# Sums formed in the up stage, a seventh raw tile, and the in projection's small matmuls set apart in stages

## The chip, the cores and the metric

The kernel runs on one core of a Trainium2 chip. The metric is the device time of one execution in microseconds; times are compared as medians of several runs. The engines are TensorE (PE, with its weight loads PEld), VectorE (DVE), ScalarE (ACT), GpSimd (POOL), and SyncE (SP), whose queue issues most of the DMAs.

## What is computed

One inference step of a decoder layer in float32, for 512 prompt tokens and 64 sample tokens (8 sequences of 8), model width 2048:

```python
h = rms_norm(x, norm1)
proj = h @ w_in                       # 2048 x 7168
ya = gate_b * causal_dwconv(gate_c * xa)                 # short convolution, 512 columns
yb = dilated_attention(...)           # 3 groups x 4 heads x 128, windows 128/512/2048, dilations 1/4/16
yc = multiscale_pool(...)             # 4 groups x 256, trailing means over 2/4/8/16, a map per group
x = x + concat(ya, yb, yc) @ w_out
h2 = rms_norm(x, norm2)
x = x + (silu(causal_dwconv(h2 @ w_gate)) * (h2 @ w_up)) @ w_down     # D_FF = 5504
y = rms_norm(x, final_norm)
```

The sample tokens also read caches of keys and values (to 2048 rows per sequence), pool and convolution states, and the updated caches and states are outputs too.

## The kernel before

**Layout.** Activations stand transposed: 128 channels on the partitions, 576 tokens (512 + 64) along the free dimension, in two halves of 288. Each float32 operand is split into a high part (rounded to the matmul's format, by ScalarE) and a low part (the rest, by VectorE); a product is the sum of three matmuls, high by high, high by low and low by high, each 128 x 128 by 128 x 288. `wload` (L146) and `split_w` (L930) split weights so.

**In projection** (up to about 880 us). `project` (L180) makes one block of 128 columns in two units of eight k-tiles, 48 matmuls each, and calls `tick` (L656) after each unit. `tick` runs the functions that `post(delay, fn)` (L644) has put on that tick, then lets two queues of generators go on, the sample tokens' scores (L473) and values (L530). Four heads of nine blocks each run (`head_tiles`, L673), with four pooling blocks behind the second and third head (`pool_tiles`, L727) and twelve blocks of the short convolution at the end. One tick after a head's last block `att_prompt` (L381) is written out whole: for each of four query tiles scores, mask, softmax, transposes, values, transpose. A pooling block is followed one tick later by its state rows (`state_rows`, L718) and, every second block, by `pool_map` (L771), whose operands are `dtl` tiles split into slots "ek", which the sample keys use too. The pool state is loaded right before its transpose (L737). The sample values are summed by `collect` (L566): a group of small matmuls into a PSUM bank, and VectorE adds the bank to `ob` (L572, L574). PSUM has two "ps" banks, one "s" and one "pt" for all these small things, and two accumulators `acc`.

**Out projection** (to about 1120 us), then **gate and up** with `strassen_steps` (L968): a 2 x 2 block product made with seven half-size products instead of eight. Each of the seven steps forms its weight combination, splits it and multiplies; four raw weight tiles are loaded (b11, b12, b22, b21), b11 and b12 are overwritten by combinations (L990, L998, L1005) and b21 by GpSimd (L1009). Raw tiles come in turn from two pools of three (`raw_tile`, L924). Of 43 column blocks, a pair of gate blocks is made, convolved and passed through silu in pieces (`later`, `go_on`), then the pair's up blocks multiply it (`up_steps`, L1252), and the result goes to memory (`act_d`). For the first five pairs also the sums that the down projection's blocks want as operands are formed and stored (`sums`, L1260).

**Down projection** (about 2060 to 2575 us). The 40 first blocks of D_FF are taken in four chunks of ten. A chunk multiplies its operands (11, s12, own, s34; 18 slots of the activations' buffers) with eight pairs of output columns, 8 x 7 products of 15 matmuls. While it runs, the pieces of the next chunk's operands are made: `first_pieces` (L1285) for the first chunk, from stored sums; `act_pieces` (L1421) for the others, from the activations themselves, loaded into six `al` tiles, with the sums formed there by VectorE (L1445, L1446, L1452). `PIECE_DUE` (L40) says after which step of the 50-odd a piece comes. The slots of two chunks overlap: some of the next chunk's pieces go into slots that the running chunk's last block frees. The last three blocks of D_FF and the final norm end the kernel.

**Order.** A list scheduler lays out each engine's order from a simulated timeline, in the order of the program where it has a choice; `high_priority` (L977) and `tc.add_manual_dep` shift it. An engine works its queue in order, and so does SP with its DMAs.

## Time and profile before

| | us |
|---|---|
| median of 3 runs (2645.61 to 2650.98) | 2648.74 |
| the profiled execution | 2641.39 |
| its span, first to last instruction | 2639.5 |
| TensorE busy (share of the span) | 2551.3 (97%) |
| VectorE busy | 1920.6 (73%) |
| ScalarE busy | 972.1 (37%) |
| GpSimd busy | 622.8 (24%) |
| mean granted TensorE clock | 0.988 |

The profile is one execution. Busy time of TensorE is that of its matmul records, which overlap and whose ends are modelled, so a busy stretch is not one at its best rate; some records can be missing. Rows by stretch give for each engine the busy time and the number of instructions, the granted clock (1.00 is 2.4 GHz, 0.50 is 1.2 GHz), the share of time in which the DMA engines were busy, and GB/s. A wait "A <- B" means that A's engine stood idle until B was done.

### The profile page before, as it was taken

To read this page: it belongs to the slowest core of one execution; us is meant where nothing else is said; L and a number is where in the kernel's file an instruction comes from. 1 tells how busy PE (TensorE), PEld (TensorE's weight loads), DVE (VectorE), ACT (ScalarE), POOL (GpSimd) and SP (SyncE) were. 2 spreads that over 40 slices of the span, in tenths; PEclk is the share of its full clock that TensorE was granted. 3 is DMA by queue.
4 is the path that set the end of the run, shared out by engine and by line. 5 is a ranking of instruction groups with operands and counts; after the bars stand their busy time and mean duration, and the time that the engine had idled before them with its cause. 6 is when DMAs were issued, how large, how long until landed. Compare 5 with 4: busy or idle time off the path is not lost.

```text
span 2639.5 us, 48741 instructions
## 1 busy us (share of the span) xinstructions
PE 2551.3 (97%) x19855; PEld 2495.6 (95%) x19855; DVE 1920.6 (73%) x2619; ACT 972.1 (37%) x1445; POOL 622.8 (24%) x460
## 2 busy tenths in 40 slices
PE   8999989989999999999999999999999999989997
PEld 7999889989989999999999999999999998989897
DVE  5667766865766544597878787877777888888875
ACT  6121221222121233354444444444444544444445
POOL 0434334434443000022222121212121111101014
PEclk9999989989999999999999999999999999999999
DMA  8547457537655696556555555555555865555534
GB/s 272 140 122 182 134 148 194 164 110 197 167 152 168 179 281 196 162 181 194 172 185 157 177 153 169 161 166 161 169 162 175 286 183 152 148 147 168 160 100 150
DMA packets 608210, 451.47 MB, mean 171 GB/s; under 512 B 22967, under 2 KB 570082, under 8 KB 601586
## 3 DMA queue, kind: packets, MB, share of 16 engines
q1 hardware_dynamic: 591358, 438.72, 56.0%
q10 hardware_dynamic: 16628, 9.64, 1.2%
q8 instruction: 156, 2.56, 0.4%
q14 instruction: 68, 0.56, 0.1%
HBM read 402.75 MB, written 132.81 MB: 203 GB/s over the span
## 4 chain that ended last, share of the span: by engine, by line
PE 83%; DVE 8%; DMA 6%; issue 1%; ACT 1%; SPq 0%; POOL 0%; DVEq 0%; ACTq 0%
PE a L945 27%; PE acc L176 11%; PE acc L178 10%; PE acc L177 10%; PE pt L945 7%; PE s L945 6%; PE b L945 6%; DMA ev<-in_cache_kv_w_dram 2%; DVE wl L934 2%; DMA al<-act 1%; DVE av L594 1%; DVE xs L1456 1%; DMA wr<-in_w_down_dram 1%; DVE wl L153 1%; PE ps L569 1%
## 5 line engine op out<-in xcount | busy, mean ns | idle before, releaser
L945 PE MATMUL a<-xs,wh 128*128 128x288 f32 x4032 | 814.4, 296 | 14.2 <-ACT wh L933 8.4
L945 PEld LDWEIGHTS a<-xs,wh 128*128 128x128 f32 x4032 | 647.7, 189 | 21.0 <-ACT wh L933 10.7
L176 PE MATMUL acc<-xs,wh 128*128 128x288 f32 x2208 | 663.4, 301 | 0.0
L177 PE MATMUL acc<-xs,wh 128*128 128x288 f32 x2208 | 657.1, 298 | 0.4 <-DVE xs L203 0.3
L178 PE MATMUL acc<-xs,wl 128*128 128x288 f32 x2208 | 655.9, 297 | 0.2 <-DVE wl L153 0.2
L945 PE MATMUL a<-xs,wl 128*128 128x288 f32 x2016 | 592.6, 295 | 1.6 <-DVE wl L934 1.6
L933 ACT ACTIVATE wh<-wr 128x1024 fp32r<-128x1024 f32 (+1 forms) x300 | 276.7, 924 | 519.7 <-PE a L945 210.9
L176 PEld LDWEIGHTS acc<-xs,wh 128*128 128x128 f32 x2208 | 417.5, 189 | 8.4 <-issue 7.6
L178 PEld LDWEIGHTS acc<-xs,wl 128*128 128x128 f32 x2208 | 419.5, 190 | 4.4 <-issue 3.9
L177 PEld LDWEIGHTS acc<-xs,wh 128*128 128x128 f32 x2208 | 418.5, 190 | 1.7 <-DVE xs L200 0.6
L945 PEld LDWEIGHTS a<-xs,wl 128*128 128x128 f32 x2016 | 378.5, 188 | 2.9 <-DVE wl L934 2.7
L1009 POOL TENSOR_TENSOR wx<-wx,wr 128x1024 f32<-128x1024 f32 (+1 forms) x75 | 161.7, 2157 | 883.3 <-DVE wl L934 747.7
L152 ACT ACTIVATE wh<-wr 128x1024 fp32r<-128x1024 f32 (+1 forms) x150 | 155.4, 1037 | 581.7 <-PE acc L177 505.3
L934 DVE TENSOR_TENSOR wl<-wr,wh 128x1024 fp32r<-128x1024 f32 (+1 forms) x300 | 316.1, 1055 | 73.1 <-ACT wh L933 70.0
L934 DVE TENSOR_TENSOR wl<-wx,wh 128x1024 fp32r<-128x1024 f32 (+1 forms) x225 | 273.8, 1223 | 84.7 <-ACT wh L933 84.5
L153 DVE TENSOR_TENSOR wl<-wr,wh 128x1024 fp32r<-128x1024 f32 (+1 forms) x150 | 242.7, 1619 | 105.5 <-ACT wh L152 99.1
L933 ACT ACTIVATE wh<-wx 128x1024 fp32r<-128x1024 f32 (+1 forms) x225 | 206.5, 921 | 169.7 <-PE b L945 85.9
L945 PE MATMUL s<-xs,wh 128*128 128x288 f32 x1024 | 208.0, 295 | 0.0
L945 PE MATMUL b<-xs,wh 128*128 128x288 f32 x1008 | 206.7, 296 | 0.3
L945 PE MATMUL pt<-xs,wh 128*128 128x288 f32 x992 | 203.1, 297 | 3.7 <-ACT wh L933 3.7
L499 POOL TENSOR_TENSOR eq<-qb,ek 128x1024 f32<-128x1024 f32 x48 | 123.1, 2565 | 224.7 <-DMA ek<-in_cache_kv_w_dram 104.4
L499 POOL TENSOR_TENSOR prod<-qb,ek 128x1024 f32<-128x1024 f32 x48 | 122.7, 2557 | 189.6 <-PE acc L176 102.6
(321 smaller groups left out, 3662.5 us busy)
## 6 DMA issues: line engine op xcount, KB each, us to landing
out_dram<-in_cache_kv_w_dram SPq DMA_DIRECT2D x320, 204.0 KB
wr<-in_w_in_dram SPq DMA_DIRECT2D x110, 512.0 KB
ek<-in_cache_kv_w_dram SPq DMA_DIRECT2D x52, 512.0 KB
ev<-in_cache_kv_w_dram SPq DMA_DIRECT2D x52, 512.0 KB
wx<-in_w_gate_dram SPq DMA_DIRECT2D x43, 512.0 KB
wr<-in_w_gate_dram SPq DMA_DIRECT2D x43, 512.0 KB
wr<-in_w_up_dram SPq DMA_DIRECT2D x43, 512.0 KB
wx<-in_w_up_dram SPq DMA_DIRECT2D x43, 512.0 KB
```

The costliest lines, as they stand in the source:

```text
L152: nc.scalar.activation(hi[:, :n], dst, AF.Copy)
L153: low.tensor_sub(lo[:, :n], dst, hi[:, :n].bitcast(F32))
L176: mark.append(nc.tensor.matmul(o, wh, xh, start=first, stop=False))
L177: nc.tensor.matmul(o, wh, xl, start=False, stop=False)
L178: nc.tensor.matmul(o, wl, xh, start=False, stop=last)
L499: with_unit(nc.gpsimd.tensor_mul(pv_, c["q"], keys))
L569: nc.tensor.matmul(o[32 * j:32 * j + 32, :P], pm[:, c:c + 32], rhs, start=i < 4, stop=i >= len(terms) - 4, tile_position=(0, 32 * j), skip ...
L594: i_ = nc.vector.scalar_tensor_tensor(av[:, t, :], v[:, t, :], w, av[:, t, :], op0=ALU.mult, op1=ALU.add)
L933: nc.scalar.activation(hi[:, :n], src, AF.Copy)
L934: nc.vector.tensor_sub(lo[:, :n], src, hi[:, :n].bitcast(F32))
L945: mm = nc.tensor.matmul(o, a[:, ws], b, start=first and k == 0 and i == 0, stop=k == n - 1 and i == 2, skip_group_check=True)
L1009: nc.gpsimd.tensor_sub(b21[:, :w], b21[:, :w], b11[:, :w])
```

## The change

Two groups of edits. In the in projection: the prompt attention of a head becomes seven steps on seven ticks, each with one part of up to four query tiles; state rows come two ticks and the pool map three ticks behind their tile; the pool state is loaded one tile ahead; `collect` leaves PSUM by a ScalarE copy. In gate, up and down: sums are formed and stored for all four chunks' pairs; the pieces of every chunk are made by kind from stored sums, through a fixed number of loads ahead; b21's combination is written into b11; the down projection has seven raw tiles (three and four) and five `al` tiles; the order of first steps at a chunk's start is shifted by one; a queue of pending pieces is no longer emptied after each up pair.

```diff
-PIECE_DUE = (4, 8, 12, 16, 19, 22, 25, 28, 31, 34, 37, 40, 46, 47, 47, 48, 49, 50, 51)
+PIECE_DUE = (2, 5, 8, 11, 14, 17, 20, 23, 27, 31, 35, 39, 42, 45, 46, 48, 50)
...
-        for T in range(4):
+        st = [{} for _ in range(4)]
+
+        def scores_(T):
...
+        def turned(T):
+            sb, c0 = st[T]["sb"], st[T]["c0"]
             pt = ps_tile("pt")
...
+        def values_(T):
+            pT, rl, c0 = st[T]["pT"], st[T]["rl"], st[T]["c0"]
             o = ps_tile()
...
+        def out(T):
+            ob, off = st[T]["ob"], T * P
             ot = ps_tile()
...
+        def step(i):
+            for k, fn in ((3, out), (2, values_), (1, turned), (0, scores_)):
+                if 0 <= i - k < 4:
+                    fn(i - k)
+
+        return [lambda i=i: step(i) for i in range(7)]
...
             if fresh[0]:
-                nc.vector.tensor_copy(ob, o[:, :P])
+                nc.scalar.copy(ob, o[:, :P])
             else:
-                nc.vector.tensor_add(ob, o[:, :P], ob)
+                part = at.tile([P, P], F32, tag="part", bufs=2, name=nm("part"))
+                nc.scalar.copy(part, o[:, :P])
+                nc.vector.tensor_add(ob, part, ob)
...
-            att_prompt(h, q, k, vn, yb)
-            have["y"] = yb
+            for i, step in enumerate(att_prompt(h, q, k, vn, yb)):
+                post(1 + i, step)
+            post(8, lambda: have.update(y=yb))
...
             if (g, s) == (2, 2):
-                post(1, prompt)
+                prompt()
...
+        def load_state():
+            if todo:
+                j = todo.pop(0)
+                nat[j] = at.tile([120, P], F32, tag="spn", bufs=2, name=nm("sp_nat"))
+                dma(nat[j], rows_in[:, j * P:(j + 1) * P])
+
+        load_state()
...
-                sp_nat = at.tile([120, P], F32, tag="ob", bufs=2, name=nm("sp_nat"))
-                dma(sp_nat, rows_in[:, j * P:(j + 1) * P])
+                sp_nat = nat.pop(j)
+                load_state()
...
-                post(1, lambda sst=sst, rows=rows: state_rows(sst, 120, [(rows, 0, 120)]))
+                post(2, lambda sst=sst, rows=rows: state_rows(sst, 120, [(rows, 0, 120)]))
                 if c:
-                    post(1, lambda gi=gi, dsl=dsl: pool_map(gi, dsl))
+                    post(3, lambda gi=gi, dsl=dsl: pool_map(gi, dsl))
...
-    wx = [wxs.enter_context(tc.tile_pool(name="weights2", bufs=1, side="right", reuse_waits="tile")), 1024]
+    wx = [wxs.enter_context(tc.tile_pool(name="weights2", bufs=1, side="right", reuse_waits="tile")), 1024, 3]
...
-        if rawn[0] % 2:
+        if rawn[0] % (wx[2] + 3) in (1, 3, 5):
             return wp.tile([P, 1024], F32, tag="wr", name=nm("wr"))
-        return wx[0].tile([P, wx[1]], F32, tag="wx", bufs=3, name=nm("wx"))
+        return wx[0].tile([P, wx[1]], F32, tag="wx", bufs=wx[2], name=nm("wx"))
...
-        b22 = load(1, 1) if late else b22
+        if late:
+            b22 = load(1, 1)
+            yield
         b21 = load(1, 0)
...
-        nc.gpsimd.tensor_sub(b21[:, :w], b21[:, :w], b11[:, :w])
+        nc.gpsimd.tensor_sub(b11[:, :w], b21[:, :w], b11[:, :w])
...
-            hl = split(w, b21[:, :w])
+            hl = split(w, b11[:, :w])
         product(a, hl, c["22"], False)
...
-             for i in range(DCHUNK)]
+             for i in range(NDC * DCHUNK)]
...
-        if ff < 2 * DCHUNK:
+        if ff < 2 * NDC * DCHUNK:
             sums(ff // 2, g1, g2)
...
-    def first_pieces(X, n):
...
+    def act_pieces(X, c, tile_, dma_, ahead_):
+
+        n = DCHUNK
+        k0 = 2 * n * c
+        todo = [(kind, i) for kind in ("11", "s12", "own", "s34") for i in range(n)]
...
+        def load11(i):
+            t = tile_()
+            for k in range(i, min(i + 2, n)):
+                part = t[:, (k - i) * HALF:(k - i + 1) * HALF]
+                dma_(part, act_d[k0 + 2 * k][:, :HALF])
+                raw["11", k] = part
+
+        def load(kind, i):
+            t = raw[kind, i] = tile_()
+            r = n * c + i
+            dma_(t, {"s12": sum_d[r][0], "own": act_d[k0 + 2 * i + 1], "s34": sum_d[r][1]}[kind])
...
+        load_to(ahead_)
         yield
...
+        for j, (kind, i) in enumerate(todo):
+            src = raw[kind, i]
...
+            with_unit(nc.scalar.activation(d0, src, AF.Copy))
+            nc.vector.tensor_sub(d1, src, d0.bitcast(F32))
+            del raw[kind, i]
+            done_ = loads.index((kind, i - i % 2 if kind == "11" else i)) + (kind != "11" or i % 2 or i + 1 == n)
+            load_to(done_ + ahead_)
             yield
...
             advance(begun[2][2], 2)
+            advance(begun[0][2], 1)
+            advance(begun[2][2], 1)
...
                 for _ in up_steps(*ups.pop(0)):
                     pass
-                go_on(len(later))
...
-    nxt = first_pieces(nextX, DCHUNK)
+    nxt = act_pieces(nextX, 0, work, dma, 8)
...
-    wx[:] = [ctx.enter_context(tc.tile_pool(name="weights3", bufs=1, side="right", reuse_waits="tile")), DCHUNK * P]
+    wx[:] = [ctx.enter_context(tc.tile_pool(name="weights3", bufs=1, side="right", reuse_waits="tile")), DCHUNK * P, 4]
+    rawn[0] = 0
...
-    AL = 6
+    AL = 5
...
-            nxt = act_pieces(nextX, f0 + nf, DCHUNK)
+            nxt = act_pieces(nextX, ci + 1, al_tile, dma_paced, AL)
...
-            pairs.append(strassen_steps(load, X, add_to(m), split_w, DCHUNK, urgent=m < 4,
-                                        late=m == 2))
+            pairs.append(strassen_steps(load, X, add_to(m), split_w, DCHUNK, urgent=m < 4))
...
+        next(pairs[0])
         for steps in pairs:
```

## Rows read from the trace of the kernel before

**Rows 1.** page, part 1: busy time, share of the span, instructions of each engine.
```profile
PE 2551.3 (97%) x19855; PEld 2495.6 (95%) x19855; DVE 1920.6 (73%) x2619; ACT 972.1 (37%) x1445; POOL 622.8 (24%) x460
```

**Rows 2.** busy time by stretch: gate and up products.
```profile
core 0: us, PE busy (x) PEld busy (x) DVE busy (x) ACT busy (x) POOL busy (x), PEclk, DMA share, GB/s
1600.00:2000.00 400.00, 400.00 (x3021) 399.77 (x3020) 308.89 (x378) 174.88 (x222) 90.25 (x90) 1.00 0.55 167
```

**Rows 3.** busy time by stretch: in projection's three stretches with idle time.
```profile
296.00:400.00 104.00, 92.34 (x835) 84.47 (x837) 67.73 (x119) 23.74 (x40) 33.55 (x25) 0.92 0.45 129
520.00:580.00 60.00, 50.06 (x500) 44.22 (x499) 39.51 (x77) 14.70 (x27) 16.32 (x14) 0.89 0.38 111
724.00:792.00 68.00, 60.22 (x641) 54.28 (x642) 47.53 (x79) 13.47 (x25) 29.68 (x17) 0.95 0.56 150
```

**Rows 4.** busy time by stretch: sum over the in projection's seven pieces at half clock.
```profile
sum 37.40, PE 30.90 PEld 26.65 DVE 30.01 ACT 7.86 POOL 10.33; mean PE 4.41 PEld 3.81 DVE 4.29 ACT 1.12 POOL 1.48
```

**Rows 5.** waits of TensorE, whole span: who for whom, us, times, longest.
```profile
PE acc L176 <- DVE ec L671: 5.3, 2, 3.8
PE ps L569 <- DVE os L574: 5.0, 1, 5.0
PE pt L411 <- ACT sb L406: 4.2, 3, 2.4
...
PE ps L739 <- DMA sp_nat<-in_state_pool_dram: 3.5, 2, 2.6
```

**Rows 6.** busy time by stretch: down projection, chunk interiors and ends in turn.
```profile
2101.00:2198.00 97.00, 93.48 (x683) 90.70 (x682) 84.72 (x129) 42.75 (x68) 13.86 (x7) 1.00 0.60 178
2198.00:2231.70 33.70, 27.98 (x180) 27.05 (x181) 26.56 (x43) 12.09 (x19) 3.12 (x2) 0.90 0.53 161
2231.70:2324.50 92.80, 90.00 (x662) 87.78 (x661) 80.69 (x121) 41.46 (x66) 11.71 (x6) 1.00 0.52 151
2324.50:2358.00 33.50, 27.51 (x176) 26.22 (x177) 26.97 (x43) 12.17 (x19) 2.54 (x2) 0.90 0.57 170
2358.00:2451.00 93.00, 90.27 (x666) 88.26 (x664) 80.84 (x122) 41.53 (x66) 12.29 (x7) 1.00 0.50 146
2451.00:2482.00 31.00, 26.28 (x185) 24.75 (x186) 25.88 (x41) 12.52 (x20) 2.37 (x2) 1.00 0.58 190
```

**Rows 7.** timeline at a chunk's end: start, duration, instruction, idle before and releaser.
```profile
2207.34 0.46 DVE L1445 TENSOR_TENSOR al<-al,al 128x288 f32<-128x288 f32 x1 [1.18 <-DMA al<-act]
...
2210.35 0.40 PE L945 MATMUL pt<-xs,wl 128*128 128x288 f32 x1 [2.38 <-DVE wl L934]
```

**Rows 8.** timeline in a chunk's interior, and line 1456: durations min/median/max.
```profile
2135.47 2.03 POOL L1009 TENSOR_TENSOR wx<-wx,wr 128x640 f32<-128x640 f32 x1 [12.98 <-DVE wl L934]
...
2135.98 2.13 DVE L1456 TENSOR_TENSOR xs<-al,xs 128x576 fp32r<-128x576 f32 x1
...
L1456 DVE TENSOR_TENSOR xs<-al,xs x45: 739/749/2128, 2121.0 to 2463.0; 128x576 fp32r<-128x576 f32 x45
```

**Rows 9.** lines 1452 and 1445, sums in the down projection: durations min/median/max.
```profile
L1452 DVE TENSOR_TENSOR al<-al,al x15: 740/749/759, 2133.8 to 2461.5; 128x576 f32<-128x576 f32 x15
...
L1445 DVE TENSOR_TENSOR al<-al,al x15: 444/459/1783, 2091.2 to 2417.8; 128x288 f32<-128x288 f32 x15
```

**Rows 10.** line 574, sums of the sample values: durations min/median/max.
```profile
L574 DVE TENSOR_TENSOR os<-ps,os x20: 273/286/292, 285.6 to 892.9; 128x128 f32<-128x128 f32 x20
```

**Rows 11.** busy time by stretch: up stage with pairs' sums, and without.
```profile
1200.00:1370.00 170.00, 170.00 (x1286) 170.00 (x1285) 139.63 (x175) 73.28 (x95) 37.68 (x39) 1.00 0.57 179
1420.00:1590.00 170.00, 170.00 (x1286) 170.00 (x1285) 132.93 (x164) 73.85 (x93) 38.01 (x40) 1.00 0.56 171
```

**Rows 12.** timeline in the up stage, GpSimd's and VectorE's queues.
```profile
1663.44 2.41 POOL L1009 TENSOR_TENSOR wx<-wx,wr 128x1024 f32<-128x1024 f32 x1 [3.22 <-issue]
...
1671.45 1.22 DVE L934 TENSOR_TENSOR wl<-wx,wh 128x1024 fp32r<-128x1024 f32 x1
...
1680.45 1.22 DVE L998 TENSOR_TENSOR wr<-wr,wr 128x1024 f32<-128x1024 f32 x1
```

114 lines of the change are left out of this document (38 added, 76 removed).

## The prediction

> **What bounds the kernel now.** I read the page's busy times first: TensorE is busy 97% of the span [rows 1], so what can be won is the time in which it stands still or runs at half clock, some 90 us in all, and the question is where that lies. The busy times by stretch answer it. In 400 us of the gate and up products TensorE is busy for all of them, 3021 matmul records, 0.1324 us each [rows 2]; that is my unit for a 128x288 product. There is nothing to win in that stage, only something to lose. The loss sits at both ends of the kernel.
>
> In the in projection three stretches hold nearly all of it: busy 92.34 of 104, 50.06 of 60 and 60.22 of 68 us [rows 3], so 29.4 us idle. TensorE's clock falls to half (1.2 of 2.4 GHz) for 37.4 us, in seven pieces that begin in or right after these idle times; it is busy for 30.9 us of that [rows 4], so about half, 15.4 us, is lost again. Together 44.8 us. The list of who waited for whom names the causes: a pool map's matmul behind VectorE's ec, the collecting matmuls of the sample values behind VectorE's os, the transposes of the attention weights behind the exponential on ScalarE, a state transpose behind its load [rows 5]. All are a short operation whose producer stands right before it.
>
> In the down projection I take the stretches as chunk interiors and chunk ends in turn and subtract the records at 0.1324 us [rows 6]. Interiors: 97.0 - 683 x 0.1324 = 6.6, then 5.2 and 4.8, together 16.6 us. Ends: 33.7 - 180 x 0.1324 = 9.9, then 10.2 and 6.5, together 26.6 us (half clock included: the first two ends are granted 0.90). At an end VectorE's queue is the story: a sum for the next chunk's operands holds it for a load of al, and the low half of a weight split, queued behind more such pieces, comes 2.38 us late for TensorE [rows 7]. In an interior it is one instruction: a low half of the activations takes 2.13 us beside a GpSimd subtraction of 2.03 us, where the median of its kind is 0.749 us [rows 8]. The product's evacuation stands behind it.
>
> **The change, part by part.** *In projection.* The attention of a head is cut into seven steps, one per half projection (48 matmuls x 0.1324 = 6.4 us), so that scores, transposes, values and output transposes of one tile are each a step apart; the longest wait of this kind in the list sums 4.2 us over three places [rows 5], well under a step. The pool map moves from one to three half projections behind its tile, the state rows from one to two, the pool state is loaded a tile ahead into a buffer of its own, and the sample sums leave PSUM by a ScalarE copy, so that the PSUM bank no longer waits until VectorE gets to it. ScalarE is at a quarter or less in these stretches [rows 3]. Nothing is computed less; 20 small copies are added on ScalarE, hidden there. Gain: between 0 (the waits come back elsewhere) and 44.8 us. I take 7 tenths, 31 us: all four large waits listed are addressed and the clock's fall hangs on them, but two maps in a row still share two accumulators, the last output transposes still wait for the sample sums, and a new order makes waits that this trace can't show.
>
> Waits added here: the one buffer for the state rows is now released a half projection later, while the next tile's copy into it stands on GpSimd. Behind that copy are the sample score products, and VectorE's reductions wait for them. At worst 8 tiles x 6.4 = 51 us of GpSimd time; it is busy for a third of the first stretch and 44% of the last [rows 3] and the order is laid out around such waits. I count it at nothing; if that fails it is the third rival.
>
> The sample sums' add now has both inputs in SBUF. With one input in PSUM it took 273 to 292 ns in all 20 cases [rows 10]. The Trainium skill (SBUF — State Buffer, Who interferes with whom) says that a VectorE instruction with two SBUF inputs and a GpSimd one that reads SBUF lock each other out for a whole instruction. The stretched activation half [rows 8] agrees with it. By the old row the 20 adds cost VectorE 5.8 us and the gain stays 31. By the rule each could be held for one more GpSimd operation, 2.03 us by [rows 8], 46 us in all on an engine that is busy 65 to 70% of these stretches [rows 3]; that would make the third rival likelier and give its time.
>
> *Up stage.* Fifteen more pairs get their sums here: three VectorE operations and two stores each. The first five pairs have them already: VectorE is busy 139.63 us in 170 with them and 132.93 without, and TensorE 170.00 in both [rows 11]. With 3.8 pairs of 44.5 us (336 matmuls) in 170, that is 1.76 us a pair, 26 us of VectorE in all, with cover of a sixth of its time. Cost nothing; without that cover 26 us. The stores stand on SP ahead of weight loads, and did so for these five pairs.
>
> The last subtraction of each strassen block now goes into the first raw tile, not the fourth. So the fourth is free earlier, and the first later: today at the end of the GpSimd subtraction, 1663.44 + 2.41 = 1665.85, then after the last split, 1671.45 + 1.22 = 1672.67 [rows 12], 6.8 us later. In this stage, with six raw tiles, that first tile becomes the next block's third, which VectorE wants at 1680.45 [rows 12]: 7.8 us are left for the load. It is 512 KB, 3.1 us at the 167 GB/s of the stage [rows 2], and up to 9.3 us if two like loads stand in front. I take the lower end, as it would be the first to be issued then: cost nothing.
>
> *Down projection.* Per chunk 15 VectorE sums go, five of 749 ns, five of 459 ns and five more of that half width [rows 9]: 5 x (0.46 + 0.46 + 0.75) = 8.3 of the 107 to 111 us that VectorE is busy per chunk [rows 6]. Operands are now loaded ready-made, 17.5 tiles a chunk for 10: some 2.2 MB more in 111 us, 20 GB/s on top of 146 to 190 [rows 6]; the up stage carries 179 with TensorE always busy [rows 11]; five buffers with a piece every three products keep about 30 us ahead. More important, pieces are made by kind: all of 11 and s12 well before the end, while the only ones that must wait for slots of the running chunk (own, s34) are needed from the fourth product of the next one. So the late low halves at a chunk end should go. The seventh raw tile gives a block's loads one tile more lead. Gain: ends 8 tenths of 26.6 = 21 us, interiors 4 tenths of 16.6 = 7 us, because the activations' low halves and the GpSimd subtraction that stretched one both stay. Together 28 us, between 0 and 43. The start of the stage, where the first chunk's pieces are made, I leave as it is.
>
> **Sum.** 31 + 28 = 59 us. From the profiled 2641.4 us: 2582. The runs' median, 2648.7, is 7.3 above that execution, and I carry that over: 2590 us.
>
> **The rivals.** *Nearly all of it*: both losses go, 88 us, 2561; against it stand the kept waits above.
>
> *Second: the down projection gives nothing.* VectorE is busy for 85% of a chunk [rows 6] and twice the load instructions go through SP and five buffers; if a late load holds VectorE's queue as al's sum does today [rows 7], the waits come back. Then only the in projection's 31: 2618.
>
> *Third: the in projection gives nothing.* The small matmuls are spaced but the queues that feed them (VectorE, GpSimd behind the state rows) are late for other reasons: far sums and score products. Then only 28: 2621.
>
> *Fourth, slower: the late raw tile.* The next block's third load lands after VectorE wants it, VectorE stands, and splits and evacuations behind it slip, in every one of 43 blocks. The wait costs 59 us, all of the gain, from 1.4 us a block on; at 2 us it costs 86 and the kernel takes 2676. For it: six loads' worth of queue on SP and copies of the caches between them; against it: VectorE has a fifth of its time free there [rows 2].
>
> *Fifth: it does not do what it says.* The instruction order is laid out by a list scheduler from a simulated timeline, so distance in the program need not be distance on the chip, and gains and new waits cancel: 2649.
>
> **How the numbers follow.** Forecast 0.55; nearly all 0.08; second 0.13; third 0.11; slower 0.07; nothing 0.06. The likeliest gives 2590, of itself 2577 to 2608. The range takes in the second and third and half of the first: 2565 to 2630. A change within 0.2%, 5 us, can't be told from none here. Faster 0.87, same 0.06, slower 0.07.
>
> **What would show it.** In the profile after: the three in-projection stretches busy but for some 3 us each and the half clock gone from most of them; no wait of a state transpose for its load and none of the collecting matmuls for os; in the down projection chunks of 114 to 118 us instead of 124 to 127, with no 2 us wait at the ends; VectorE about 1.7 us busier per up pair with TensorE still full. I am wrong if TensorE shows idle time in the up stage, if new waits for loads (wr, al) stand in the down chunks, or if the pool stretches still show the half clock.

## The result, and the profile after

The changed kernel takes 2607.55 us (median of 4 runs, 2607.42 to 2615.55); the kernel before took 2647.18 in the 4 runs beside it (2645.09 to 2650.98). The ratio is 0.9856, 95% interval 0.9834 to 0.9879: 1.4% faster, some 38 us. The forecast was 2590, range 2565 to 2630. The profiled execution took 2607.47 us and spans 2605.5, against 2641.39 and 2639.5 before, so 34.0 us of span are to be accounted for.

I cut both spans at the same products, from the start times of their records: the first product of the gate stage, the first of the down projection, the last of the down projection.

| us of span | before | after | gain | forecast |
|---|---|---|---|---|
| to the first gate product (in and out projection) | 1118.5 | 1110.0 | 8.5 | 31 |
| gate and up | 962.6 | 965.1 | -2.5 | 0 |
| down projection | 493.9 | 466.2 | 27.7 | 28 |
| the rest | 64.5 | 64.2 | 0.3 | 0 |
| all | 2639.5 | 2605.5 | 34.0 | 59 |

The down projection came out almost to the microsecond, the in projection gave a quarter of its term. The first line of the page, busy times of the whole span after the change (compare [rows 1]):

```profile
PE 2533.1 (97%) x19855; PEld 2484.6 (95%) x19855; DVE 1955.0 (75%) x2615; ACT 970.7 (37%) x1469; POOL 663.5 (25%) x460
```

The operations are nearly as many as before (VectorE 2615 for 2619, GpSimd 460 for 460), yet VectorE is busy 34.4 us longer and GpSimd 40.7. Something stretches them; this comes back below.

Busy time by stretch after, the three stretches of the in projection of [rows 3] and one more, 640 to 680, in which TensorE had been busy for all 40 us before. Columns: busy time (and instructions) of PE, PEld, DVE, ACT, POOL, then granted clock, DMA share, GB/s. The first line is that fourth stretch before, the block under it is after.

```profile
640.00:680.00 40.00, 40.00 (x302) 39.73 (x301) 36.13 (x36) 7.67 (x11) 23.81 (x10) 1.00 0.68 183
```

```profile
296.00:400.00 104.00, 97.52 (x930) 90.82 (x930) 71.94 (x122) 26.38 (x47) 32.96 (x25) 0.98 0.46 132
520.00:580.00 60.00, 54.51 (x559) 48.70 (x552) 40.04 (x77) 16.13 (x31) 20.39 (x17) 0.97 0.36 103
640.00:680.00 40.00, 33.01 (x232) 32.49 (x232) 33.06 (x42) 7.09 (x11) 20.85 (x9) 0.91 0.54 147
724.00:792.00 68.00, 55.95 (x605) 51.22 (x604) 49.98 (x79) 13.80 (x26) 28.91 (x17) 0.92 0.57 163
```

The first two are better (idle 6.5 and 5.5 us instead of 11.7 and 9.9), the third is worse (12.1 instead of 7.8), and a hole of 7 us is new. The half clock of this stage, 37.4 us before [rows 4], is 23.9 us, and 17.1 of it lies in the last two stretches. The waits of TensorE after, whole span (us, times, longest), to hold against [rows 5]:

```profile
PE s L391 <- DVE sb L402: 12.1, 1, 12.1
PE pt L417 <- ACT sb L408: 6.4, 3, 4.4
PE ps L568 <- DVE mb L565: 6.4, 1, 6.4
...
PE a L979 <- DVE wl L968: 4.2, 4, 3.3
```

Three of the four waits of [rows 5] are gone from this list: the pool map's for ec, the collecting matmuls' for os, the state transpose's for its load; the fourth, the attention transposes' for the exponential, went from 4.2 to 6.4 us. In their place stand one of 6.4 us that the kernel before didn't have (mb) and one of 12.1 us where it had 2.7: the scores of the prompt attention (L391) wait until VectorE has emptied the one "s" bank (L402). The timeline of TensorE, GpSimd and VectorE there (start, duration, instruction, idle before and releaser):

```profile
721.47 2.41 POOL L520 TENSOR_TENSOR prod<-qb,ek 128x1024 f32<-128x1024 f32 x1 [2.49 <-DVE st L521]
721.52 3.45 DVE L153 TENSOR_TENSOR wl<-wr,wh 128x1024 fp32r<-128x1024 f32 x1
...
722.04 0.46 PE L391 MATMUL s<-t,t 128*32 128x128 f32 x8
...
730.14 2.19 DVE L617 SCALAR_TENSOR_TENSOR av<-ev,st,av 128x128 f32<-128x128 f32 x8 [4.98 <-DMA ev<-in_cache_kv_w_dram]
...
733.38 4.01 DVE L617 SCALAR_TENSOR_TENSOR av<-ev,st,av 128x128 f32<-128x128 f32 x7
...
733.59 2.34 POOL L520 TENSOR_TENSOR eq<-qb,ek 128x1024 f32<-128x1024 f32 x1 [9.71 <-DMA kvd<-ns]
...
739.11 1.91 DVE L617 SCALAR_TENSOR_TENSOR av<-ev,st,av 128x128 f32<-128x128 f32 x7
740.95 1.21 DVE L153 TENSOR_TENSOR wl<-wr,wh 128x1024 fp32r<-128x1024 f32 x1
742.08 0.27 DVE L399 SCALAR_TENSOR_TENSOR sb<-cst,s 128x128 f32<-128x128 f32 x1
742.28 0.41 DVE L402 SCALAR_TENSOR_TENSOR sb<-cst,s 128x256 f32<-128x256 f32 x1
...
742.83 1.09 PE L391 MATMUL s<-t,t 128*32 128x256 f32 x8 [12.05 <-DVE sb L402]
```

The scores that started at 722.04 lie in the bank for 20 us. VectorE could empty it in 0.7 us, but has other work queued ahead of it: the sample values (L617), which wait 4.98 us for a load of ev, reductions and a weight split. Two of these operations run beside a GpSimd score product and take 3.45 and 4.01 us, where L153 elsewhere in this timeline takes 1.21 and seven operations of L617 take 1.91. A stage of distance, 6.4 us, is no help against a queue that is 20 us late.

In the down projection, busy time by stretch: first the second chunk before, then the first three chunks after; the chunks of before measured 123.1, 126.6 and 126.4 us ([rows 6] shows their parts):

```profile
2204.00:2331.00 127.00, 118.38 (x845) 115.22 (x844) 107.76 (x165) 53.66 (x84) 14.83 (x8) 0.97 0.53 155
```

```profile
2075.00:2196.00 121.00, 115.30 (x839) 113.66 (x839) 102.68 (x153) 54.47 (x87) 15.41 (x8) 0.97 0.74 232
2196.00:2312.00 116.00, 114.08 (x847) 112.24 (x846) 101.16 (x150) 53.37 (x85) 15.54 (x8) 1.00 0.63 187
2312.00:2427.00 115.00, 113.07 (x839) 111.23 (x838) 100.08 (x149) 53.28 (x84) 15.43 (x8) 1.00 0.62 186
```

The clock is full in the second and third, VectorE has some 7 us less to do per chunk, TensorE's idle time is 1.9 us a chunk.

### The profile page after: what moved, and what is told of

It reads as the page before. It is cut to its first block, busy times and chain, and to the rows that moved or that the text cites. A ratio compares the mean times of both kernels' runs of the same rounds, so it can differ in the third digit from the quotient of the medians.

```text
span 2605.5 us, 48931 instructions
## 1 busy us (share of the span) xinstructions
PE 2533.1 (97%) x19855; PEld 2484.6 (95%) x19855; DVE 1955.0 (75%) x2615; ACT 970.7 (37%) x1469; POOL 663.5 (25%) x460
## 4 chain that ended last, share of the span: by engine, by line
PE 83%; DVE 7%; DMA 5%; issue 1%; POOL 1%; ACT 1%; SPq 0%; DVEq 0%; ACTq 0%; POOLq 0%
PE a L979 28%; PE acc L176 10%; PE acc L177 9%; PE acc L178 9%; PE b L979 7%; PE pt L979 7%; PE s L979 7%; DMA ek<-in_cache_kv_w_dram 1%; DVE wl L968 1%; DMA ev<-in_cache_kv_w_dram 1%; DVE av L617 1%; POOL prod L520 1%; DVE wl L153 1%; DVE ec L783 1%; PE ps L590 1%
## 5 line engine op out<-in xcount | busy, mean ns | idle before, releaser
L176 PE MATMUL acc<-xs,wh 128*128 128x288 f32 x2208 | 662.5, 301 | 0.3 <-ACT t L814 0.3
L967 ACT ACTIVATE wh<-wr 128x1024 fp32r<-128x1024 f32 (+1 forms) x312 | 299.0, 960 | 500.6 <-PE a L979 166.0
L176 PEld LDWEIGHTS acc<-xs,wh 128*128 128x128 f32 x2208 | 415.5, 188 | 9.6 <-issue 8.0
L968 DVE TENSOR_TENSOR wl<-wr,wh 128x1024 fp32r<-128x1024 f32 (+1 forms) x312 | 351.6, 1128 | 58.2 <-ACT wh L967 57.0
L152 ACT ACTIVATE wh<-wr 128x1024 fp32r<-128x1024 f32 (+1 forms) x150 | 155.4, 1036 | 576.6 <-PE acc L177 523.6
L1045 POOL TENSOR_TENSOR wr<-wx,wr 128x1024 f32<-128x1024 f32 (+1 forms) x52 | 157.4, 3026 | 765.3 <-DVE wl L968 669.3
L153 DVE TENSOR_TENSOR wl<-wr,wh 128x1024 fp32r<-128x1024 f32 (+1 forms) x150 | 224.5, 1497 | 113.9 <-ACT wh L152 111.7
L968 DVE TENSOR_TENSOR wl<-wx,wh 128x640 fp32r<-128x640 f32 (+1 forms) x213 | 250.6, 1180 | 36.9 <-ACT wh L967 35.1
L967 ACT ACTIVATE wh<-wx 128x640 fp32r<-128x640 f32 (+1 forms) x213 | 183.2, 865 | 146.2 <-PE a L979 37.0
L979 PEld LDWEIGHTS s<-xs,wh 128*128 128x128 f32 x1024 | 164.1, 188 | 4.1 <-ACT wh L967 2.5
```

The lines of the kernel that those rows point to most:

```text
L152: nc.scalar.activation(hi[:, :n], dst, AF.Copy)
L153: low.tensor_sub(lo[:, :n], dst, hi[:, :n].bitcast(F32))
L176: mark.append(nc.tensor.matmul(o, wh, xh, start=first, stop=False))
L967: nc.scalar.activation(hi[:, :n], src, AF.Copy)
L968: nc.vector.tensor_sub(lo[:, :n], src, hi[:, :n].bitcast(F32))
L979: mm = nc.tensor.matmul(o, a[:, ws], b, start=first and k == 0 and i == 0, stop=k == n - 1 and i == 2, skip_group_check=True)
```

## The experiments

All times are ratios to the kernel before, run beside each kernel on the same chip, with their 95% interval; the changed kernel has 0.9856. Diffs are against the changed kernel. The stages in us, cut as above (in five kernels with the changed kernel's in projection untouched, the first gate product came between 1106.2 and 1111.4, so a few us there mean little):

| | ratio | first gate product | gate and up | chunks 1 to 3 | last chunk and blocks |
|---|---|---|---|---|---|
| before | 1 | 1118.5 | 962.6 | 123.1, 126.6, 126.4 | 117.8 |
| changed | 0.9856 | 1110.0 | 965.1 | 121.3, 115.4, 115.4 | 114.2 |
| e1_down_only | 0.9905 | 1117.4 | 967.1 | 120.2, 115.4, 115.4 | 114.2 |
| e2_in_only | 0.9955 | 1109.9 | 963.2 | 123.5, 125.1, 125.5 | 118.5 |
| e3_att_whole | 0.991 | 1126.2 | 964.0 | 119.6, 115.4, 115.4 | 114.2 |
| e4_b21_place | 0.9827 | 1111.4 | 963.0 | 118.9, 114.0, 114.0 | 113.1 |
| e5_collect_vector | 0.9853 | 1104.4 | 966.2 | 120.5, 115.3, 115.3 | 114.2 |
| e6_pool_near | 0.9812 | 1094.5 | 965.6 | 119.7, 115.3, 115.6 | 114.2 |
| e7_six_raw | 1.0009 | 1106.2 | 966.0 | 131.3, 123.3, 124.2 | 120.3 |
| e8_by_number | 0.9863 | 1107.4 | 966.6 | 118.5, 115.8, 115.8 | 114.2 |
| e9_vector_time | 0.9937 | 1109.5 | 965.9 | 120.5, 122.0, 122.4 | 121.4 |
| e10_sums_alone | 0.9883 | 1109.4 | 962.4 | 118.9, 117.7, 120.1 | 114.5 |
| e11_scores_scalar | 0.9838 | 1112.5 | 961.7 | 118.1, 114.0, 114.0 | 113.1 |
| e12_place_near | 0.9782 | 1098.2 | 962.8 | 119.3, 114.0, 114.0 | 113.0 |

**The two halves by themselves.** e1_down_only has the in projection as before (attention whole, pool distances of one, VectorE emptying the sample sums) and the rest changed:

```diff
-            for i, step in enumerate(att_prompt(h, q, k, vn, yb)):
-                post(1 + i, step)
-            post(8, lambda: have.update(y=yb))
+            att_prompt(h, q, k, vn, yb)
+            have["y"] = yb
...
-                post(2, lambda sst=sst, rows=rows: state_rows(sst, 120, [(rows, 0, 120)]))
+                post(1, lambda sst=sst, rows=rows: state_rows(sst, 120, [(rows, 0, 120)]))
...
-                    post(3, lambda gi=gi, dsl=dsl: pool_map(gi, dsl))
+                    post(1, lambda gi=gi, dsl=dsl: pool_map(gi, dsl))
...
```

> The in projection as before, everything from the up stage on as changed. Theory A (the two halves add, and the trace's split of the 34 us gained is right: 8 in the in projection, 28 in the down projection, 2 lost in the up stage): 25 us faster than before, some 2622 us, chunks of 115 us. Rival (part of the down projection's gain comes with the in projection's shift in time): 15 us or less, 2632 or more.

Measured 2618.28 us, ratio 0.9905 [0.989, 0.992]: 25 us faster than before. e2_in_only has the opposite: the in projection changed, the rest as before.

```diff
-        nc.gpsimd.tensor_sub(b11[:, :w], b21[:, :w], b11[:, :w])
+        nc.gpsimd.tensor_sub(b21[:, :w], b21[:, :w], b11[:, :w])
...
-        if ff < 2 * NDC * DCHUNK:
+        if ff < 2 * DCHUNK:
...
-    def act_pieces(X, c, tile_, dma_, ahead_):
+    def first_pieces(X, n):
...
```

> The in projection as changed, everything else as before. Theory A: 8 us faster than before, some 2639 us, TensorE waits of 6 and 12 us for VectorE again in the third and fourth head. Rival (the recorded prediction: those waits are an accident of the other half's order): 25 to 31 us faster, 2616 to 2622.

Measured 2631.57 us, 0.9955 [0.9939, 0.9972]: 12 us. The two add up to the whole (0.0095 + 0.0045 = 0.0140 of 0.0144), so no effect of one part on the other is seen beyond the noise, and the small gain of the in projection is its own: the same waits stand in e2's list (L391 for L402 11.1 us, L568 for L565 6.4 us).

**Are the stages worth nothing?** If small matmuls late for other reasons are the whole story, the prompt attention can stand on one tick again, at the distances of the rest.

```diff
-        return [lambda i=i: step(i) for i in range(7)]
+        for T in range(4):
+            scores_(T)
+            turned(T)
+            values_(T)
+            out(T)
...
-            for i, step in enumerate(att_prompt(h, q, k, vn, yb)):
-                post(1 + i, step)
-            post(8, lambda: have.update(y=yb))
+            def whole():
+                att_prompt(h, q, k, vn, yb)
+                have["y"] = yb
+            post(1, whole)
```

> The changed kernel, but with each head's prompt attention written out whole on one tick as before; pool distances, state loads ahead and the ScalarE copies kept. Theory A (VectorE is late behind loads of cached values, and distance in the program does not cure that): within 6 us of the changed kernel, 2602 to 2614. Rival 1 (the stages took away the 9 us of attention waits and their half clock, as predicted): 10 or more slower, 2618 or more. Rival 2 (the stages do harm: the scores' single bank now holds TensorE): 10 or more faster, 2597 or less.

Measured 2619.12 us, 0.991 [0.9895, 0.9925]; the first gate product comes 16 us later than in the changed kernel. Its list of TensorE's waits:

```profile
PE s L391 <- DVE sb L402: 12.5, 1, 12.5
PE acc L176 <- DVE ec L698: 10.1, 2, 6.4
```

So the stages are worth some 16 us, and something else in this half of the change costs about half of that: without them the first gate product comes 7.7 us later than in the kernel before.

**Where b21's combination is written.** e4_b21_place puts GpSimd's subtraction back into b21, seven raw tiles kept:

```diff
-        nc.gpsimd.tensor_sub(b11[:, :w], b21[:, :w], b11[:, :w])
+        nc.gpsimd.tensor_sub(b21[:, :w], b21[:, :w], b11[:, :w])
...
-            hl = split(w, b11[:, :w])
+            hl = split(w, b21[:, :w])
```

> The changed kernel, but GpSimd's last combination is written into b21 again, not into b11. Theory A (that swap is what makes VectorE 6 us in 170 busier and GpSimd's subtraction 3.0 us for 2.2, and what costs the up stage its 2.4 us): VectorE near 140 us of 170 in the up stage again, the up stage back to full, down projection the same, 2605. Rival (the swap frees a raw tile early enough to matter in the down projection): chunks longer by 2 us or more each, 2611 or more.

Measured 2597.39 us, 0.9827 [0.9811, 0.9844], 0.3% below the changed kernel: some 8 us, 2.1 in gate and up and 6.3 in the down projection by the table. Neither theory had the 6.3, and what makes the chunks shorter there was not traced. Why gate and up gain is seen in the rows of two lines, 1411 to 1991 us: the third operation of a pair's sums (L1307) and the subtraction (L1045); durations are min/median/max in ns. First the changed kernel, then e4_b21_place:

```profile
L1307 DVE TENSOR_TENSOR wk<-wk,wk x13: 2953/2966/2971, 1411.0 to 1946.9; 128x576 f32<-128x576 f32 x13
...
L1045 POOL TENSOR_TENSOR wr<-wx,wr x26: 3257/3266/3276, 1410.0 to 1968.9; 128x1024 f32<-128x1024 f32 x26
```

```profile
L1307 DVE TENSOR_TENSOR wk<-wk,wk x14: 749/751/754, 1410.9 to 1990.7; 128x576 f32<-128x576 f32 x14
...
L1045 POOL TENSOR_TENSOR wx<-wx,wr x27: 2391/2795/2813, 1411.1 to 1991.0; 128x1024 f32<-128x1024 f32 x27
```

And the changed kernel's timeline at one of these places:

```profile
1676.25 3.26 POOL L1045 TENSOR_TENSOR wr<-wx,wr 128x1024 f32<-128x1024 f32 x1 [16.34 <-DVE wl L968]
...
1676.03 1.22 DVE L968 TENSOR_TENSOR wl<-wx,wh 128x1024 fp32r<-128x1024 f32 x1
1677.16 2.96 DVE L1307 TENSOR_TENSOR wk<-wk,wk 128x576 f32<-128x576 f32 x1
```

The subtraction starts inside a VectorE operation that ends at 1677.25, and takes 0.86 us longer than its 2.41 of before [rows 12]; the next VectorE operation ends 0.6 us after the subtraction does, though it needs 0.75. Each looks as if it stood while the other ran. The Trainium skill (SBUF — State Buffer, Who interferes with whom) says just that of a VectorE operation with two SBUF inputs and a GpSimd one that reads SBUF; the trace agrees, with 2.2 us lost by VectorE in each of 13 cases. The moved destination let the subtraction begin one VectorE operation earlier: in e4_b21_place it starts at the same place at 1678.65 us, when L1307 has been running since 1678.43. The busy time of VectorE in 170 us of the up stage: 132.93 before without sums [rows 11], then the changed kernel, then e4_b21_place:

```profile
1411.00:1581.00 170.00, 170.00 (x1286) 170.00 (x1285) 145.71 (x173) 73.72 (x95) 46.02 (x40) 1.00 0.60 183
```

```profile
1411.00:1581.00 170.00, 170.00 (x1286) 170.00 (x1285) 137.09 (x170) 74.23 (x94) 41.70 (x40) 1.00 0.59 181
```

The sums themselves cost 4.2 us, the swap 8.6 more.

**What made the down projection faster?** Three candidates: the order by kind, VectorE's saved time, the seventh raw tile. The new due steps, the five `al` tiles and the order of first steps at a chunk's start were not tried by themselves. e8_by_number keeps the stored sums but takes the pieces in the old order, by block number (only the last four stand in another order), from the second chunk on:

```diff
         todo = [(kind, i) for kind in ("11", "s12", "own", "s34") for i in range(n)]
+        if c:
+            todo = [(kind, i) for i in range(n - 2) for kind in ("11", "s12", "own", "s34")]
+            todo += [(kind, i) for i in (n - 2, n - 1) for kind in ("11", "s12")]
+            todo += [(kind, i) for i in (n - 2, n - 1) for kind in ("own", "s34")]
```

> The changed kernel, but from the second chunk on the pieces come by number as before (11, s12, own, s34 of one pair, then of the next), still from stored sums. Theory O (the order did it: what needs the running chunk's slots is now wanted only by the fourth product of the next chunk): the waits of some 2 us and the half clock at the chunk ends are back, chunks of 121 to 125 us instead of 115, 18 to 25 us slower than the changed kernel. Theory V (it was VectorE's time for the sums): chunks within 1.5 us of 115, within 5 us of the changed kernel.

Measured 2604.22 us, 0.9863 [0.9848, 0.9879], chunks of 115.8: as good. The order is not it. e9_vector_time keeps the order and gives VectorE about as much work back as the sums took, by forming the low half of the five s34 pieces of a chunk three times:

```diff
             nc.vector.tensor_sub(d1, src, d0.bitcast(F32))
+            if c and kind == "s34":
+                nc.vector.tensor_sub(d1, src, d0.bitcast(F32))
+                nc.vector.tensor_sub(d1, src, d0.bitcast(F32))
```

> The changed kernel, but each s34 piece's low half is formed three times over, so 10 operations of 0.75 us, 7.5 us a chunk, are given back to VectorE in chunks two to four, near the 8.3 us of sums taken away. Theory V: chunks of 120 us or more, 12 to 20 us slower than the changed kernel. Theory O: within 5 us of it, chunks within 1.5 us of 115.

Measured 2624.19 us, 0.9937 [0.9919, 0.9956]. The first chunk keeps its 120.5 us, the others go to 122.0, 122.4 and 121.4, and the half clock is back at the chunk ends. Its second and third chunk by stretch, against 1.00 and 1.9 us idle in the changed kernel:

```profile
2196.00:2318.00 122.00, 116.71 (x842) 114.62 (x841) 106.74 (x159) 53.27 (x84) 20.28 (x8) 0.97 0.59 176
2318.00:2440.00 122.00, 117.60 (x839) 115.39 (x838) 106.35 (x158) 53.27 (x84) 19.50 (x8) 0.96 0.58 176
```

VectorE is busy 5.6 us longer in the second chunk (106.74 for 101.16), GpSimd 4.7 us in as many operations (20.28 for 15.54), and the chunks take 6 to 7 us longer. The added work thus lengthens GpSimd's operations as well; what part of the loss is due to that was not separated. e7_six_raw takes the seventh raw tile away and, as before, loads the second pair's third tile late; all else is as changed:

```diff
-    wx[:] = [ctx.enter_context(tc.tile_pool(name="weights3", bufs=1, side="right", reuse_waits="tile")), DCHUNK * P, 4]
+    wx[:] = [ctx.enter_context(tc.tile_pool(name="weights3", bufs=1, side="right", reuse_waits="tile")), DCHUNK * P, 3]
...
-            pairs.append(strassen_steps(load, X, add_to(m), split_w, DCHUNK, urgent=m < 4))
+            pairs.append(strassen_steps(load, X, add_to(m), split_w, DCHUNK, urgent=m < 4,
+                                        late=m == 2))
```

> The changed kernel, but with six raw weight tiles in the down projection and the second pair's third tile loaded late, as before. If the seventh tile matters: waits for weight loads on VectorE and 1 to 3 us more per chunk, 4 to 12 us slower than the changed kernel. If the pieces alone carry the gain: within 3 us of it.

Measured 2643.47 us, 1.0009 [0.9999, 1.0019] over 10 runs: the whole gain is gone, some 40 us where 4 to 12 were expected. e10_sums_alone has six tiles too, but the subtraction in place; against the old kernel's down projection it has the stored sums, the order by kind and the small edits named above. Its edit is that of e4 and that of e7 together:

```diff
-        nc.gpsimd.tensor_sub(b11[:, :w], b21[:, :w], b11[:, :w])
+        nc.gpsimd.tensor_sub(b21[:, :w], b21[:, :w], b11[:, :w])
...
-            pairs.append(strassen_steps(load, X, add_to(m), split_w, DCHUNK, urgent=m < 4))
+            pairs.append(strassen_steps(load, X, add_to(m), split_w, DCHUNK, urgent=m < 4,
+                                        late=m == 2))
```

> The changed kernel with b21's combination in place again and six raw tiles in the down projection, as before: what is left of the second half are the stored sums and the order of the pieces. Theory V (VectorE's time for the sums bounded the chunks, and the seventh tile only pays for the swap, which holds b11 longer): chunks of 114 to 117 us, within 6 us of the version with b21 in place and seven tiles, a ratio to before of 0.982 to 0.986. Rival (the seventh tile is needed by itself): chunks of 121 us or more, 20 us slower, a ratio of 0.990 or more.

Measured 2610.17 us, 0.9883 [0.9863, 0.9903], between the two expectations: with six tiles instead of seven (e4, 0.9827) it loses 0.0056, 15 us, 11.2 of them in the down projection by the table. VectorE's waits for raw tiles in the down projection tell the kernels apart. In the changed kernel none stands in the list; the longest of the kernel before, then e7_six_raw, then e10_sums_alone:

```profile
DVE wr L998 <- DMA wr<-in_w_down_dram: 9.7, 4, 3.4
```

```profile
DVE wx L1041 <- DMA wr<-in_w_down_dram: 32.7, 23, 3.1
...
DVE wr L1034 <- DMA wr<-in_w_down_dram: 12.6, 4, 4.4
```

```profile
DVE wr L1034 <- DMA wr<-in_w_down_dram: 9.6, 3, 4.5
DVE wx L1041 <- DMA wr<-in_w_down_dram: 7.6, 11, 1.7
```

So the late raw tile is real: 45.3 us of VectorE's time with the swap and six tiles, 17.2 without the swap, nothing with seven. With the subtraction in place six tiles still give 22.7 of the 33.9 us that the down projection gains with seven; with the swap they give nothing (499.1 us for the stage, 493.9 before). So the seventh tile is worth a third of the gain by itself, and all of it once the swap is there.

**What costs in the in projection?** e5_collect_vector lets VectorE empty the sample sums' bank as before:

```diff
-                nc.scalar.copy(ob, o[:, :P])
+                nc.vector.tensor_copy(ob, o[:, :P])
...
-                part = at.tile([P, P], F32, tag="part", bufs=2, name=nm("part"))
-                nc.scalar.copy(part, o[:, :P])
-                nc.vector.tensor_add(ob, part, ob)
+                nc.vector.tensor_add(ob, o[:, :P], ob)
```

> The changed kernel, but the sample sums leave PSUM by VectorE as before. Theory A (the ScalarE copy takes away the wait of 5 to 7 us of the collecting matmuls for os, and no more): that wait is back, 4 to 8 us slower than the changed kernel. Rival (the new 6 us wait for mb and 12 us wait for the scores' bank in the third and fourth head come with the copy): these are gone and it is as fast or faster.

Measured 2601.59 us, 0.9853 [0.9838, 0.9869]: no different from the changed kernel. The collecting matmuls wait again,

```profile
PE ps L590 <- DVE os L595: 5.5, 1, 5.5
```

but the 12 us wait of the scores is down to 0.2 us (the one for mb stays, 6.3). One late stretch of VectorE is paid once, at whichever bank TensorE meets first. e11_scores_scalar tries the same on the scores: ScalarE copies them out of the bank, and a yield more stands ahead of L568 (with e4's subtraction, so e4 is what it is held against).

```diff
-            nc.vector.scalar_tensor_tensor(sb[:, c0:256], cst[:, C_G0 + c0:C_G0 + 256], ch, s[:, c0:256],
+            nc.scalar.copy(sb[:, c0:], s[:, c0:])
+            nc.vector.scalar_tensor_tensor(sb[:, c0:256], cst[:, C_G0 + c0:C_G0 + 256], ch, sb[:, c0:256],
...
-                                           s[:, 256:].rearrange("p (g x) -> p g x", g=2),
+                                           sb[:, 256:].rearrange("p (g x) -> p g x", g=2),
...
+        yield
...
```

> The version with b21 in place, and in the in projection two edits more: ScalarE copies the prompt scores out of their PSUM bank before VectorE adds the mask, and one more step lies between the samples' maximum and its transpose. Theory B (TensorE waits because a bank is held until a VectorE that is late behind loads gets to it): the waits of 12 us for the scores' bank and of 6 us for mb are gone with their half clock, 12 to 22 us faster than that version, a ratio of 0.974 to 0.978. Rival (VectorE's lateness just comes out at the next place, as when the sample sums were given back to it): within 5 us, a ratio of 0.981 to 0.985.

Measured 2597.86 us, 0.9838 [0.9819, 0.9857], against 0.9827 [0.9811, 0.9844] for e4: no gain. Its list has neither of the two new waits, and this in their place:

```profile
PE pt L418 <- ACT sb L409: 23.6, 6, 10.5
PE acc L176 <- DVE ec L696: 7.1, 2, 4.4
```

The bank is free, and the next reader of VectorE's work, the transpose behind the exponential, waits instead. e6_pool_near asks about the pool's distances, put back to one:

```diff
-                post(2, lambda sst=sst, rows=rows: state_rows(sst, 120, [(rows, 0, 120)]))
+                post(1, lambda sst=sst, rows=rows: state_rows(sst, 120, [(rows, 0, 120)]))
                 if c:
-                    post(3, lambda gi=gi, dsl=dsl: pool_map(gi, dsl))
+                    post(1, lambda gi=gi, dsl=dsl: pool_map(gi, dsl))
```

> The changed kernel, but state rows and pool map one tick behind their tile as before. Theory A (the distance took away the pool maps' waits for ec and ek and half clock there): 8 to 15 us slower than the changed kernel, a ratio to before of 0.989 to 0.992. Rival (loads ahead and copies did it, or the waits come out elsewhere): within 4 us, a ratio of 0.984 to 0.987.

Measured 2591.67 us, 0.9812 [0.9796, 0.9829]: 0.44% faster than the changed kernel, some 12 us, which neither theory had. The first gate product comes at 1094.5, 24.0 us before the old kernel's. GpSimd's waits from 500 to 900 us, in the kernel before, the changed kernel and e6_pool_near:

```profile
POOL prod L499 <- DMA ek<-in_cache_kv_w_dram: 35.0, 4, 20.3
```

```profile
POOL prod L520 <- DMA ek<-in_cache_kv_w_dram: 42.8, 4, 32.6
...
POOL sst L787 <- PE ps L745: 6.5, 1, 6.5
```

```profile
POOL prod L520 <- DMA ek<-in_cache_kv_w_dram: 24.6, 2, 20.2
```

The map's operands lie in the two "ek" slots that the sample keys are loaded into. The rows of that tile, 560 to 660 us, tell when the last map is done with them (601.6 and 579.6 us), and GpSimd's timeline when the next score product on those slots runs, first in the changed kernel, then in e6_pool_near:

```profile
L178 PE MATMUL acc<-ek,wl x16: 291/294/299, 563.9 to 601.6; 128*128 128x288 f32 x16
...
611.16 2.40 POOL L520 TENSOR_TENSOR prod<-qb,ek 128x1024 f32<-128x1024 f32 x1 [32.63 <-DMA ek<-in_cache_kv_w_dram]
```

```profile
L178 PE MATMUL acc<-ek,wl x8: 294/295/300, 575.7 to 579.6; 128*128 128x288 f32 x8
...
587.74 2.41 POOL L520 TENSOR_TENSOR prod<-qb,ek 128x1024 f32<-128x1024 f32 x1 [20.22 <-DMA ek<-in_cache_kv_w_dram]
```

With two more half projections of distance the slots come free 22 us later; the keys come late, GpSimd stands 32.63 us, waits for keys again up to 645 us, and from there five score products follow one another without a gap, with VectorE's reductions behind them, while TensorE waits 6.4 us for mb, to 656 us. In e6_pool_near that wait is gone and TensorE is busy for all of the stretch:

```profile
640.00:680.00 40.00, 40.00 (x323) 39.07 (x322) 32.00 (x42) 8.69 (x14) 14.54 (x6) 1.00 0.59 163
```

Held against each other by the start of the same product of L176, e6_pool_near is 7.3 us ahead of the changed kernel at 641 us of the latter and 16.7 us at 677. So the wait for mb and the half clock behind it (6.8 us from 653.8) make some 9 us of the gain; where the 7.3 us before it come from was not traced. The state rows' buffer, the other distance, shows in one wait: the copy into it (L787) stands 6.5 us for the transpose of the tile before (L745), and not at all in e6_pool_near. What each of the two distances costs was not separated.

**Both losses taken out.** e12_place_near joins the edits of e4 and e6:

```diff
-                post(2, lambda sst=sst, rows=rows: state_rows(sst, 120, [(rows, 0, 120)]))
+                post(1, lambda sst=sst, rows=rows: state_rows(sst, 120, [(rows, 0, 120)]))
...
-                    post(3, lambda gi=gi, dsl=dsl: pool_map(gi, dsl))
+                    post(1, lambda gi=gi, dsl=dsl: pool_map(gi, dsl))
...
-        nc.gpsimd.tensor_sub(b11[:, :w], b21[:, :w], b11[:, :w])
+        nc.gpsimd.tensor_sub(b21[:, :w], b21[:, :w], b11[:, :w])
...
-            hl = split(w, b11[:, :w])
+            hl = split(w, b21[:, :w])
```

> The changed kernel with two things put back: GpSimd's subtraction is written in place (b21) again, and the state rows and the pool map follow at a distance of one stage again. Theory A: the two losses lie in different stages (in the in projection the pool's products come behind a VectorE that is late; in the up and down stages the subtraction takes VectorE's and GpSimd's time) and add up: ratio to before 0.9856 - 0.0044 (near pool) - 0.0029 (in place) = 0.978, about 2586 us; the gate stage begins at about 1094 us, the first block's gate to the first down product takes 964 us or less, the chunks of the down stage 118.9, 114.0, 114.0 and 113.1. Theory B: the near pool's gain was a chance placing of the half-clock stretches in one kernel and doesn't carry over: gate begins at about 1110 and the ratio is 0.983, that of the kernel in place alone.

Measured 2584.94 us (5 runs, 2580.32 to 2587.54), 0.9782 [0.9765, 0.9799], the fastest of all: 2.2% below the kernel before. The two losses lie in different stages and add up, as expected. The 9.3 us wait of L391 for L402 is still in its list.

## Why the prediction was right or wrong

**The bound** was read rightly: all of the gain lies at the two ends, and the up stage could only lose.

**In projection, 31 forecast, 8.5 measured: the mis-sized term.** Three steps went into it. That the listed waits would go held for three of four. That stages make up for a short producer right ahead held too (e3: 16 us worse without them for the prompt attention). The step that failed is "waits added here": I looked for what the longer distances hold, found the state rows' buffer and counted it at nothing, and didn't see the other one, though the sharing of the "ek" slots was in front of me in the code: the pool map three ticks behind its tile holds slots that GpSimd's queue wants. In GpSimd's waits it is the larger: 18.2 us more for ek than in e6, against 6.5 at the state rows' buffer. With the distances at one (e6) the stage gains 24.0 us, in e12 20.3: most of what I had put down, from the other edits alone. That is 0.45 to 0.54 of the 44.8 us, where I took 0.7, and the pool's distances had the wrong sign. The third rival named this mechanism (queues late for other reasons, score products) and was about half right: the waits were not removed where VectorE itself was late, they moved. The ScalarE copy of the sample sums, which I counted among the four remedies, is worth nothing (e5), and the lists say that the same lateness is then paid at the "s" bank.

**The sample sums' adds** were to take 5.8 us, or up to 46 in all if each were held for a GpSimd operation. Seventeen of the 20 took 267 to 291 ns as in [rows 10], three took 1.26, 2.17 and 2.42 us: 10.6 us in all. By the timeline 15 of them met no GpSimd operation under way. Of the five that did, the three long ones ended some 0.15 us after it; beside the other two it was GpSimd's operation that was long, 2.67 us where five of the six other operations of its kind took 1.28 to 1.30.

**Up stage, 0 forecast, -2.5 measured.** The sums cost less than I had put down, 4.2 us in 170 (e4 against [rows 11]) for 6.7, and were hidden: TensorE is busy for all 170. The swap at no cost was wrong, though not through what I weighed. I priced it by the lateness of the first raw tile and took the lower end. The 7.8 us that I left for its load were a misreading: the first to read the next block's third tile is not L998 at 1680.45 but, in the kernel before,

```profile
1677.44 1.22 DVE L1005 TENSOR_TENSOR wx<-wr,wx 128x1024 f32<-128x1024 f32 x1
```

so 4.8 us were left. VectorE does wait for that load now, at just this line (L1041), in 16 of 26 blocks, in the changed kernel from 1411 to 1991 us

```profile
DVE wx L1041 <- DMA wr<-in_w_up_dram: 13.9, 11, 2.2
...
DVE wx L1041 <- DMA wr<-in_w_gate_dram: 7.1, 5, 2.4
```

21 us, 0.8 a block, below the 1.4 from which I let the slower rival decide, and the free time of VectorE (a seventh in 1411 to 1581) takes most of it. What I had not priced is that another place for the subtraction is another neighbour in time, and that VectorE and GpSimd lengthen each other there (e4). In all the swap costs about 8 us.

**Down projection, 28 forecast, 27.7 measured, for half the reasons.** "More important, pieces are made by kind" fell: in the old order the chunks are as short (e8). What carries the gain is VectorE's time (e9: 5.6 us back on VectorE, 6 to 7 us lost, half clock at the ends again) and the seventh raw tile, which I had passed over in one sentence as "one tile more lead": without it 15 us go (e10), and all of the gain with the swap beside it (e7). The saving of VectorE was 7 us a chunk, where I had 8.3. The 17.5 loads a chunk, the second rival's ground, make no wait of ScalarE or VectorE for al: none stands in their lists. The end of 28 was reached with the swap's 6 us against it; without the swap it is 33.9 (e4). That the sum came out within 0.3 us is luck.

**The slower rival** has its mechanism where I hadn't put it, in the down projection; it costs its price only with six tiles: 32.7 us of L1041's wait and a time equal to before. The seventh tile is what keeps it away.

**The offset.** I carried 7.3 us from the profiled execution to the median; after the change the two agree within 0.1 us. That brought the forecast of 2590 nearer to the measured 2607.55 than the sum was, by luck. The profiled executions alone give 2607.47 against the 2582 of my sum: 25 us, of which the in projection is 22.5 and the up stage 2.5.

**What was to show it.** Chunks of 114 to 118 us: yes from the second on. Three stretches idle for 3 us each: no, 6.5, 5.5 and 12.1. VectorE 1.7 us busier per up pair: (145.71 - 132.93) / 3.8 = 3.4, the swap included. Of the signs of being wrong one came: the pool stretches still show the half clock. VectorE has no new waits for wr or al in the down chunks (ScalarE waits for raw tiles once 1.9 and once 1.7 us), and TensorE's idle time in the up stage is 0.6 us in 400 (1591 to 1991).

## What to carry to other kernels

Distance in the program helps where a producer is short and only just late; before lengthening one, list every buffer that the moved step keeps alive and ask which queue waits for it. Where an in-order engine is late by more than the distance, moving its consumers or emptying one bank elsewhere only chooses who waits: the lateness has to go (in the down projection: less work for VectorE, a tile more for its loads). An operation on GpSimd that is given another place or another moment is to be priced with its VectorE neighbours, even if the count of operations stays the same.

## What the hardware showed that was not expected

A VectorE subtraction of 128x576 that takes 0.75 us alone took 2.95 to 2.97 us in all 13 cases in which it met a GpSimd subtraction of 128x1024 already begun, and the GpSimd subtraction took 3.26 us for 2.41: a fixed price, not a scatter. And the half clock comes back with small causes: in e9_vector_time 5.6 us more of VectorE per chunk brought granted clocks of 0.97 and 0.96 for 1.00 over whole chunks.
